# Second attention with score products of 64 rows: two maps side by side instead of stacked halves

## The chip, the cores and the metric

The kernel runs on one core of one Trainium2 chip. The metric is the device time of one execution in microseconds; the time before is 2244.63 us, the median of three runs (2244.57 to 2247.15).

## The reference

Two layers over 1024 tokens of width 1024, in float32. The first layer mixes tokens with latent attention, the second with differential attention; each mixer and each feed-forward block is followed by a layer norm. The change touches the differential attention alone:

```python
# 8 heads, two maps (m) of 64 columns each, values of 128 columns
q = q.reshape(b, s, 8, 2, 64); k = k.reshape(b, s, 8, 2, 64); v = v.reshape(b, s, 8, 128)
logits = einsum('bqhmd,bkhmd->bmhqk', q_b, k) * 64 ** -0.5 - slopes * dist      # then the chunk mask
p = softmax(logits)
a = p[:, 0] - lam * p[:, 1]
o = einsum('bhqk,bkhe->bqhe', a, v)
```

The mask lets a query see its own chunk of 64 tokens and all earlier ones.

## The kernel before, in words

Products of float32 numbers are made from "hi" and "lo" parts in the type fp32r: a number is cast (hi, on ScalarE), the rest is what the cast lost (lo, on VectorE), and a product is hi·hi + hi·lo + lo·hi. Most of the kernel is projections and feed-forward products of this kind with 128 rows and 512 columns.

The second attention is the `with ExitStack() as st` block from about line 1536 on. `attention` walks over 64 blocks, a head `h` and 128 queries `i` each, the last head in the order `LAST_ORDER`. For each it calls the scores two blocks ahead (`score_b`), then the transposes of the probabilities (`turn_b`), and after every second block the product with the values (`mix_b`). Other work is spread between by slot numbers (`at`, `fill`): the projections of the next head (`proj_b`, tile `bp`), values (`values_b`, tile `bv`), norms, and the first products of the output projection (`zp_a`). The order on each engine is then made by a planner, which runs a timeline of its own and takes the priorities of `tc.high_priority` into account; `behind(i, j)` holds two instructions of one engine in a given order.

`proj_b` makes 512 columns of the queries or keys of one head: 24 products into a bank of tag `m` (two banks), rows 0 to 63 for map 0 and 64 to 127 for map 1. The split out of this bank differs for queries and keys:

- Queries (L1592 to L1596): for each map, ScalarE casts its 64 rows into a tile of its own, VectorE makes the lo rows, and a DMA issued by GpSimd copies the 64 hi rows to the other 64 rows of the tile. So each map has a tile with hi in both halves, and a tile (`ql`) with lo in one half and zeros in the other. The zeros come once from DRAM (`zero_dr`, L1552), where the first attention stored them (`store_zeros`, L1492 and L1493).
- Keys (L1602, L1603): for each map, ScalarE casts its 64 rows into its own rows of the map's tile, and VectorE writes the lo part into the other 64 rows.

`score_b` then calls `softmax_block` once for each map. With n = 128(i+1) keys, in one bank of tag `s` where n is 512 or less and in two banks of n/2 columns where it is more, each bank takes two products of 128 rows (L241): [hi; hi] with [hi; lo], and [lo; 0] with the same keys. VectorE then adds the distances out of the bank and takes the row's bound (L244), ScalarE takes the exponential with its sum (L247), VectorE the reciprocal (L249). GpSimd scales map 1 (L1617) and VectorE joins the two maps (L1618). Three banks have the tag `s`, two `m`, two `t` (transposes), one `o`.

Of the kernel before, what the change touches and what calls it, by code (L numbers as in the profile page):

```python
# [9 lines left out]
F32 = mybir.dt.float32  # L10
F32R = mybir.dt.float32r
AF = mybir.ActivationFunctionType
ALU = mybir.AluOpType
# [3 lines left out]
P = 128  # L17
S = 1024
# [16 lines left out]
BIGF = 3.0e38  # L35
# [7 lines left out]
def trunk(  # L43
# [32 lines left out]
    nc = tc.nc  # L76
    V, A, G, T = nc.vector, nc.scalar, nc.gpsimd, nc.tensor
# [9 lines left out]
    wp = ctx.enter_context(tc.tile_pool(name="wp", bufs=3))  # L87
# [13 lines left out]
    dr = ctx.enter_context(tc.tile_pool(name="dr", bufs=1, space=DRAM))  # L101
# [7 lines left out]
    def f32(t):  # L109
        return t.bitcast(F32)  # L110

    def big_tile(name, dt=F32R):
        return big.tile([P, 2, 1024], dt, tag="big", name=name)

    def ps_s(name):
        return ps.tile([P, 512], F32, tag="s", bufs=ps_bufs[0], name=name)

    def ps_m(name):
        return ps.tile([P, 512], F32, tag="m", bufs=ps_bufs[1], name=name)
# [14 lines left out]
    def small(name, n=1):  # L134
        return sp.tile([P, 2], F32, tag="small", name=name, bufs=22)[:, :n]
# [3 lines left out]
    def load_w(src, cols, name, hi=None, lo=None, eng=None, raw=None, after=()):  # L139

        if raw is None:
            raw = wp.tile([P, 1024], F32, tag="wr", bufs=2, name=f"r_{name}")
        newest["weight load"] = nc.sync.dma_start(raw[:, :cols], src).ins
        if hi is None:
            hi = wp.tile([P, 1024], F32R, tag="wh", name=f"h_{name}")
            lo = wp.tile([P, 1024], F32R, tag="wl", name=f"l_{name}")
        i = A.copy(hi[:, :cols], raw[:, :cols])
        j = (eng or G).tensor_tensor(lo[:, :cols], raw[:, :cols], f32(hi[:, :cols]), ALU.subtract)
        for k, key in zip((i, j), after):
            behind(k.ins, newest[key])  # L150
        newest["weight"] = i.ins
        return hi, lo
# [14 lines left out]
    def mm3(ps_out, pairs):  # L167
        n = len(pairs)
        for i, (lh, ll, rh, rl) in enumerate(pairs):
            T.matmul(ps_out, lh, rh, start=(i == 0), stop=False)  # L170
            T.matmul(ps_out, lh, rl, start=False, stop=False)  # L171
            T.matmul(ps_out, ll, rh, start=False, stop=(i == n - 1))  # L172
# [9 lines left out]
    def behind(i, j):  # L182

        tc.add_manual_dep(
            i, j.name,
            mybir.DependencyInfo(mybir.DependencyClass.NoSync, mybir.DependencyReason.DATA),
            reason="kept in program order",
        )
# [42 lines left out]
    def softmax_block(lp, q_pass, s_bias, i, scale, name):  # L231
        n = (i + 1) * P
        nb = 1 if n <= 512 else 2
        w = n // nb
        l = lp.tile([P, 1024], F32, tag="l", name=f"l_{name}")
        mx = BIGF
        for b in range(nb):
            s = ps_s(f"s_{name}_{b}")
            ks = slice(b * w, (b + 1) * w)
            for j, (lh, rh) in enumerate(q_pass):  # L240
                T.matmul(s[:, :w], lh, rh[:, ks], start=(j == 0), stop=(j == len(q_pass) - 1))  # L241
            bv = s_bias[:, 896 - P * i + b * w:896 - P * i + (b + 1) * w]
            m = small(f"mx_{name}_{b}")
            V.tensor_tensor_reduce(l[:, ks], s[:, :w], bv, -scale, mx, ALU.add, ALU.min, m)  # L244
            mx = m
        sm = small(f"sm_{name}")
        newest["exp"] = A.activation(l[:, :n], l[:, :n], AF.Exp, bias=mx, scale=-1.0, accum_out=sm).ins  # L247
        r = small(f"r_{name}")
        V.reciprocal(r, sm)  # L249
        return l, r  # L250
# [953 lines left out]

    o_dr = [dr.tile([H, P, 256], F32, name=f"o_dr_{g}") for g in range(4)]
    on_dr = dr.tile([H - 2, P, 2, S], F32, name="on_dr")
    zero_dr = dr.tile([P, 512], F32, name="zero_dr")
    wo_dr = [dr.tile([P, 2, D], F32, name=f"wo_dr{h}") for h in range(H)]
    xs_dr = [dr.tile([S, D], F32, name=f"xs_dr{l}") for l in range(3)]

# [6 lines left out]
    ba, cos, sin = (krp.tile([P, S], F32, tag=t, name=t) for t in ("ba", "cos", "sin"))  # L1217
# [7 lines left out]
    with tc.tile_pool(name="a0", bufs=2, side="right") as pool:  # L1225
# [42 lines left out]
        kt = pool.tile([P, NTB, P], F32, tag="kt", name="kt", bufs=1)  # L1268
# [84 lines left out]
    with ast as st:  # L1353
        pool = st.enter_context(tc.tile_pool(name="a1", bufs=2, reuse_waits="tile"))
        vp = st.enter_context(tc.tile_pool(name="a1v", bufs=12, side="right", reuse_waits="tile"))
        lp = st.enter_context(tc.tile_pool(name="a1l", bufs=4, side="right", reuse_waits="tile"))
# [104 lines left out]
        def at(slot, fn, *args):  # L1461
            fill.setdefault(slot, []).append(lambda: fn(*args))
# [9 lines left out]
        for h in range(1, H):  # L1472
            b = 8 * (h - 1)
# [13 lines left out]
        at(10, load_late)  # L1487
        at(12, make_late)

        def store_zeros():  # L1490
            t = wp.tile([P, 1024], F32R, tag="wl", name="zeros")
            A.copy(t[:, :512], ba[:, :512])  # L1492
            nc.sync.dma_start(zero_dr, f32(t[:, :512]))  # L1493

        at(14, store_zeros)
        first = FirstBlock(w_o_a, o_dr)
        for h in range(first.HEADS):
            at(8 * H - 8 + h // 2, first.weight, h)
        tb, n = first.tb, first.HEADS
# [37 lines left out]
    with ExitStack() as st:  # L1537
        lp = st.enter_context(tc.tile_pool(name="b1l", bufs=5, reuse_waits="tile"))
        pool = st.enter_context(tc.tile_pool(name="b1", bufs=2, reuse_waits="tile"))
        ptp = st.enter_context(tc.tile_pool(name="b1p", bufs=4, reuse_waits="tile"))  # L1540
        bb = pool.tile([P, S], F32, tag="bb", name="bb", bufs=1)
        nc.sync.dma_start(bb, c_bias_b)
        vt, lt, pts, sqs, q_slot = {}, {}, {}, {}, {}
        qt = [big_tile(f"bq{j}") for j in range(2)]
        kt = [big_tile(f"bk{j}") for j in range(2)]
        ob = big_tile("bo", F32)
        q_hi = [qt[0][:, 0], qt[0][:, 1], qt[1][:, 0]]
        q_lo = [qt[1][:, 1]] + [pool.tile([P, S], F32R, tag=f"ql{j}", name=f"ql{j}", bufs=1) for j in range(2)]
        for ql in q_lo:
            for mp in range(2):  # L1550
                b = slice(64 - mp * 64, 128 - mp * 64)
                nc.sync.dma_start(f32(ql[b, mp * 512:mp * 512 + 512]), zero_dr[b])  # L1552

        def values_b(pr, tb):
            if ("v", pr) not in wts:
# [20 lines left out]
        def proj_b(h, which, hf):  # L1576
            if (which, h) not in wts:
                wts[which, h] = load_w(w_b_qk[h, which], 1024, f"wb{h}_{which}")
            wh, wl = wts[which, h]
            hs = slice(hf * 512, hf * 512 + 512)  # L1580
            m = ps_m(f"bp{h}_{which}_{hf}")
            mm3(m, [(wh[:, k * P:k * P + P], wl[:, k * P:k * P + P], xT[0][hf][:, k, :], xT[1][hf][:, k, :])
                    for k in range(KD)])
            sc = float(2.0 ** (h + 1) / 8.0)
            if which == 0:
                j = 2 * h + (hf if h < H - 1 else 1 - hf)
                q2, ql = q_slot[h, hf] = q_hi[j % 3], q_lo[j % 3]
                for mp in range(2):
                    a = slice(mp * 64, mp * 64 + 64)
                    b = slice(64 - mp * 64, 128 - mp * 64)  # L1590
                    qh = q2[:, mp * 512:mp * 512 + 512]
                    A.activation(qh[a], m[a, :], AF.Copy, scale=sc)  # L1592
                    V.scalar_tensor_tensor(
                        ql[a, mp * 512:mp * 512 + 512], m[a, :], sc, f32(qh[a]), ALU.mult, ALU.subtract
                    )
                    nc.gpsimd.dma_start(qh[b], qh[a])  # L1596
            else:
                for mp in range(2):
                    a = slice(mp * 64, mp * 64 + 64)
                    b = slice(64 - mp * 64, 128 - mp * 64)  # L1600
                    k = kt[h % 2][:, mp]
                    A.copy(k[a, hs], m[a, :])  # L1602
                    V.tensor_tensor(k[b, hs], m[a, :], f32(k[a, hs]), ALU.subtract)  # L1603

        def score_b(h, i):
            c = slice((i % 4) * P, (i % 4) * P + P)
            n = (i + 1) * P
            (q2, ql), k = q_slot[h, i // 4], kt[h % 2]
            (l0, r0), (l1, r1) = [
                softmax_block(  # L1610
                    lp,
                    [(t[:, m * 512:m * 512 + 512][:, c], k[:, m]) for t in (q2, ql)],
                    bb, i, float(2.0 ** -(h + 1)), f"b{h}_{i}_{m}",
                )
                for m in range(2)
            ]
            G.tensor_scalar(l1[:, :n], l1[:, :n], r1, nlam, ALU.mult, ALU.mult)  # L1617
            V.scalar_tensor_tensor(l0[:, :n], l0[:, :n], r0, l1[:, :n], ALU.mult, ALU.add)  # L1618
            lt[h, i] = l0
# [73 lines left out]
        for h in range(1, H):  # L1693
            b = 8 * (h - 1)
# [22 lines left out]
        b = 8 * (H - 1) - 2  # L1717
# [104 lines left out]
```

## Time and profile before

| | before |
|---|---|
| median of three runs | 2244.63 us |
| the profiled execution | 2244.52 us |
| its span in the profile | 2242.6 us |
| TensorE matmul busy | 2227.4 us (99%) |
| VectorE, ScalarE, GpSimd busy | 1587.6, 1008.6, 883.8 us |
| second attention, first to last score product | 1115.9 to 1524.9 us |

The span runs from the first to the last instruction that the profile records; the profiled execution's own time has 1.9 us beside it. PE is a row of matmuls, PEld one of weight loads, each load going ahead of its matmul. A matmul's duration in the profile runs from its start to the end of its last result, and the next one starts before that, so the cost of a matmul in a dense stretch is the distance between two starts, not its duration.

### The profile page before, as it was taken

The numbers are of one execution on the slowest core, as the hardware profiler recorded it, in microseconds if no ns is written. First come the engines' busy times: TensorE is split into PE (matmuls) and PEld (weight loads), VectorE is DVE, ScalarE is ACT, GpSimd is POOL, SyncE is SP. The second block draws the span as 40 slices with busy tenths as digits, with TensorE's granted clock in tenths as the row PEclk, the third lists the DMA queues.
The fourth block names the chain that finished last, engine by engine and source line by source line (L and its number), as shares of the span: only waits on it lengthen the run. The fifth ranks groups of instructions, "written<-read, shape, count | busy, mean of one in ns | idle before, by whom it ended". The sixth has DMA issues, their size and how long they took to land.

```text
span 2242.6 us, 30084 instructions
## 1 busy us (share of the span) xinstructions
PE 2227.4 (99%) x10850; PEld 1878.7 (84%) x10850; DVE 1587.6 (71%) x2951; ACT 1008.6 (45%) x2082; POOL 883.8 (39%) x711
## 2 busy tenths in 40 slices
PE   9999999999999999999999999999999999999998
PEld 9888888888888888888888888888888888888887
DVE  6677776597656667768588777776597666668668
ACT  4465664342323324445466656555442233334444
POOL 2243452015434446456433434321024444446452
PEclk9999999999999999999999999999999999999999
DMA  5031335334313138544310212164444232246644
GB/s 208 15 127 64 116 108 195 125 141 151 121 71 141 71 122 333 207 173 155 118 48 34 71 45 69 47 244 146 151 153 168 74 113 99 101 151 260 238 140 158
DMA packets 107989, 295.49 MB, mean 132 GB/s; under 512 B 8512, under 2 KB 34880, under 8 KB 96576
## 3 DMA queue, kind: packets, MB, share of 16 engines
q1 hardware_dynamic: 103552, 283.87, 35.9%
q0 software_dynamic: 4000, 9.44, 1.5%
q8 instruction: 86, 1.41, 0.3%
q14 instruction: 63, 0.52, 0.1%
q10 hardware_dynamic: 288, 0.26, 0.0%
HBM read 208.86 MB, written 80.48 MB: 129 GB/s over the span
## 4 chain that ended last, share of the span: by engine, by line
PE 95%; DVE 3%; ACT 1%; issue 1%; POOL 0%; DVEq 0%; ACTq 0%; POOLq 0%
PE gb L619 16%; PE ga L619 11%; PE gc L619 11%; PE dw L972 7%; PE dx L972 5%; PE zp_a L494 4%; PE s_a L241 3%; PE zp_a L351 3%; PE dv L972 3%; PE dy L972 3%; PE s_b L241 2%; PE bv L1564 2%; PE bp L170 2%; PE bp L172 2%; PE bp L171 2%; PE hq L1282 2%
## 5 line engine op out<-in xcount | busy, mean ns | idle before, releaser
L575 ACT CAST op_g<-gr 128x512 fp32r<-128x512 f32 x240 | 147.6, 622 | 400.2 <-PE gb L619 219.6
L575 POOL TENSOR_TENSOR op_g<-gr,op_g 128x512 fp32r<-128x512 f32 x104 | 147.2, 1421 | 304.8 <-DVE tmp L733 167.5
L575 DVE TENSOR_TENSOR op_h<-rh,op_h 128x512 fp32r<-128x512 f32 x154 | 156.2, 1029 | 86.8 <-ACT op_h L575 86.6
L619 PE MATMUL ga<-xh_m,op_g 128*128 128x512 f32 x512 | 168.1, 389 | 0.0
L972 PE MATMUL dw<-op_w_t,op_h 128*128 128x512 f32 x660 | 152.4, 391 | 0.0
L972 PEld LDWEIGHTS dw<-op_w_t,op_h 128*128 128x128 f32 x660 | 123.4, 188 | 25.6 <-POOL op_w_t L575 0.2
L575 ACT CAST op_h<-rh 128x512 fp32r<-128x512 f32 x154 | 92.3, 619 | 112.3 <-PE dv L972 34.6
L247 ACT ACTIVATE l_b<-l_b,mx_b 128x256 f32<-128x256 f32 (+7 forms) x128 | 99.5, 777 | 67.7 <-DVE mx_b L244 63.6
L575 POOL TENSOR_TENSOR op_w_t<-tt,op_w_t 128x512 fp32r<-128x512 f32 x66 | 93.7, 1420 | 89.9 <-ACT op_w_t L575 82.8
L1617 POOL TENSOR_SCALAR l_b<-l_b,r_b,cst 128x128 f32<-128x128 f32 (+3 forms) x64 | 52.9, 826 | 180.3 <-DVE r_b L249 150.2
L972 PE MATMUL dx<-op_w_b,op_h 128*128 128x512 f32 x528 | 120.3, 389 | 0.0
L575 DVE TENSOR_TENSOR op_g<-gr,op_g 128x512 fp32r<-128x512 f32 x136 | 110.6, 815 | 8.8 <-ACT op_g L575 8.6
L972 PEld LDWEIGHTS dx<-op_w_b,op_h 128*128 128x128 f32 x528 | 99.1, 188 | 20.6
L575 POOL TENSOR_TENSOR op_g<-s,op_g 128x512 fp32r<-128x512 f32 x40 | 56.6, 1414 | 150.1 <-ACT op_g L575 150.1
L619 PE MATMUL gc<-t1h_f,op_g 128*128 128x512 f32 x352 | 115.5, 389 | 0.0
L619 PE MATMUL gb<-t4h_f,op_g 128*128 128x512 f32 x352 | 115.5, 389 | 0.0
L619 PE MATMUL gc<-b22h_f,op_g 128*128 128x512 f32 x352 | 115.5, 389 | 0.0
L619 PE MATMUL gb<-t3h_f,op_g 128*128 128x512 f32 x352 | 115.2, 389 | 0.0
L619 PE MATMUL gb<-t2h_f,op_g 128*128 128x512 f32 x352 | 114.9, 389 | 0.0
L619 PEld LDWEIGHTS ga<-xh_m,op_g 128*128 128x128 f32 x512 | 96.1, 188 | 20.0
L170 PE MATMUL bp<-xT_f,h_wb 128*128 128x512 f32 x256 | 103.0, 403 | 1.0 <-DVE bk L1603 0.8
L172 PE MATMUL bp<-xT_f,l_wb 128*128 128x512 f32 x256 | 101.4, 396 | 0.0
(406 smaller groups left out, 6516.4 us busy)
## 6 DMA issues: line engine op xcount, KB each, us to landing
gr<-in_w_gu SPq DMA_DIRECT2D x44, 1024.0 KB, 6.9
rh<-h_dr SPq DMA_DIRECT2D x28, 1024.0 KB, 4.9
h_dr<-sh SPq DMA_DIRECT2D x22, 1024.0 KB, 4.9
h_dr<-hp SPq DMA_DIRECT2D x22, 768.0 KB, 4.0
tt<-in_w_dn SPq DMA_DIRECT2D x22, 512.0 KB, 8.4
rh<-h_dr SPq DMA_DIRECT2D x14, 768.0 KB, 4.3
z<-xs_dr SPq DMA_DIRECT2D x16, 512.0 KB, 11.2
rw_b<-in_w_dn SPq DMA_DIRECT2D x8, 1024.0 KB, 7.2
```

The source lines that it names most:

```text
L170: T.matmul(ps_out, lh, rh, start=(i == 0), stop=False)
L171: T.matmul(ps_out, lh, rl, start=False, stop=False)
L172: T.matmul(ps_out, ll, rh, start=False, stop=(i == n - 1))
L241: T.matmul(s[:, :w], lh, rh[:, ks], start=(j == 0), stop=(j == len(q_pass) - 1))
L247: newest["exp"] = A.activation(l[:, :n], l[:, :n], AF.Exp, bias=mx, scale=-1.0, accum_out=sm).ins
L351: i = T.matmul(m, ot[:, a, h, :], wo[h][w][:, c], start=(h == 0 and (a, w) == (0, 0)), stop=(h == H - 1 and a == 1), skip_group_check=True ...
L494: T.matmul(m, a[:, h, :], self.wo[h][w][:, c], start=(start and h == heads[0] and a is oh and w == 0), stop=(stop and h == heads[-1] and a ...
L575: return A.copy(hi, src).ins, eng.tensor_tensor(lo, src, f32(hi), ALU.subtract).ins
L619: T.matmul(o, w[:, a, kc], x[b][:, k, :], start=(first and k == 0 and (a, b) == (0, 0)), stop=(k == 3 and a == 1), skip_group_check=True,)
L972: i = T.matmul(o, h[:, a, c], w[:, b_], start=(first and (a, b_) == (0, 0)), stop=(last and a == 1), skip_group_check=True,).ins
L1282: T.matmul(hq[:, :384], lh[:, kc], w[:, 0:384], start=st, stop=sp_)
L1617: G.tensor_scalar(l1[:, :n], l1[:, :n], r1, nlam, ALU.mult, ALU.mult)
```

## The change

The queries and keys of both maps are split with all 128 rows at once: one cast on ScalarE and one operation on VectorE where there were two of each, hi and lo lying side by side in the free dimension. There are no second copies of the hi rows, no copying DMAs, and no zeros.

The score products become products of 64 rows: rows 0 to 63 are map 0, rows 64 to 127 map 1. Each map takes hi·hi, hi·lo and lo·hi, so a bank takes three products in place of two. Two banks of tag `s`, one for each map, are filled together, map 1 and map 0 by turns. `behind` keeps the six products in this order, and all but the first have a raised priority, so that the planner does not put other work between them. VectorE empties both banks, and the exponentials come when both maps are through. `softmax_block` is no longer used here; its steps stand in `score_b`.

```diff
-    zero_dr = dr.tile([P, 512], F32, name="zero_dr")
...
-        def store_zeros():
-            t = wp.tile([P, 1024], F32R, tag="wl", name="zeros")
-            A.copy(t[:, :512], ba[:, :512])
-            nc.sync.dma_start(zero_dr, f32(t[:, :512]))
-        at(14, store_zeros)
...
-        q_hi = [qt[0][:, 0], qt[0][:, 1], qt[1][:, 0]]
-        q_lo = [qt[1][:, 1]] + [pool.tile([P, S], F32R, tag=f"ql{j}", name=f"ql{j}", bufs=1) for j in range(2)]
-        for ql in q_lo:
-            for mp in range(2):
-                b = slice(64 - mp * 64, 128 - mp * 64)
-                nc.sync.dma_start(f32(ql[b, mp * 512:mp * 512 + 512]), zero_dr[b])
+        qt = [t[:, :, :512] for t in qt] + [pool.tile([P, 2, 512], F32R, tag="q", name="q", bufs=1)]
...
             if which == 0:
                 j = 2 * h + (hf if h < H - 1 else 1 - hf)
-                q2, ql = q_slot[h, hf] = q_hi[j % 3], q_lo[j % 3]
-                for mp in range(2):
-                    a = slice(mp * 64, mp * 64 + 64)
-                    b = slice(64 - mp * 64, 128 - mp * 64)
-                    qh = q2[:, mp * 512:mp * 512 + 512]
-                    A.activation(qh[a], m[a, :], AF.Copy, scale=sc)
-                    V.scalar_tensor_tensor(
-                        ql[a, mp * 512:mp * 512 + 512], m[a, :], sc, f32(qh[a]), ALU.mult, ALU.subtract
-                    )
-                    nc.gpsimd.dma_start(qh[b], qh[a])
+                q = q_slot[h, hf] = qt[j % 3]
+                A.activation(q[:, 0], m, AF.Copy, scale=sc)
+                V.scalar_tensor_tensor(q[:, 1], m, sc, f32(q[:, 0]), ALU.mult, ALU.subtract)
             else:
-                for mp in range(2):
-                    a = slice(mp * 64, mp * 64 + 64)
-                    b = slice(64 - mp * 64, 128 - mp * 64)
-                    k = kt[h % 2][:, mp]
-                    A.copy(k[a, hs], m[a, :])
-                    V.tensor_tensor(k[b, hs], m[a, :], f32(k[a, hs]), ALU.subtract)
+                k = kt[h % 2][:, :, hs]
+                A.copy(k[:, 0], m)
+                V.tensor_tensor(k[:, 1], m, f32(k[:, 0]), ALU.subtract)
...
         def score_b(h, i):
...
-            (l0, r0), (l1, r1) = [
-                softmax_block(lp, [(t[:, m * 512:m * 512 + 512][:, c], k[:, m]) for t in (q2, ql)],
-                    bb, i, float(2.0 ** -(h + 1)), f"b{h}_{i}_{m}")
-                for m in range(2)
-            ]
+            for b in range(nb):
+                ks = slice(b * w, (b + 1) * w)
+                ss = [ps_s(f"s_{nm}_{m}_{b}") for m in both]
+                last = None
+                for x, y in ((0, 0), (0, 1), (1, 0)):
+                    for m in (1, 0):
+                        a = slice(64 * m, 64 * m + 64)
+                        with tc.high_priority(0 if last is None else 200):
+                            one = T.matmul(ss[m][:, :w], q[a, x, c], k[a, y, ks], start=(x + y == 0), stop=(x == 1)).ins
+                        if last is not None:
+                            behind(one, last)
+                        last = one
+                for m in both:
+                    x = small(f"mx_{nm}_{m}_{b}")
+                    V.tensor_tensor_reduce(ls[m][:, ks], ss[m][:, :w], bv, -scale, mx[m], ALU.add, ALU.min, x)
+                    mx[m] = x
+            for m in both:
+                A.activation(ls[m][:, :n], ls[m][:, :n], AF.Exp, bias=mx[m], scale=-1.0, accum_out=sm)
+                V.reciprocal(rs[m], sm)
```

More of the change, by code (lines that the diff above doesn't have):

```diff
@@ L1607, in score_b @@
             n = (i + 1) * P
-            (q2, ql), k = q_slot[h, i // 4], kt[h % 2]
-            (l0, r0), (l1, r1) = [
[L1610 to L1614, printed above, removed]
-                for m in range(2)
-            ]
+            q, k = q_slot[h, i // 4], kt[h % 2]
+            nb = 1 if n <= 512 else 2
+            w = n // nb
+            scale, nm = float(2.0 ** -(h + 1)), f"b{h}_{i}"
+            both = range(2)
+            ls = [lp.tile([P, 1024], F32, tag="l", name=f"l_{nm}_{m}") for m in both]
+            mx = [BIGF, BIGF]
+            for b in range(nb):
[10 more added lines that the diff above has]
+                        last = one
+                bv = bb[:, 896 - P * i + b * w:896 - P * i + (b + 1) * w]
+                for m in both:
+                    x = small(f"mx_{nm}_{m}_{b}")
+                    V.tensor_tensor_reduce(ls[m][:, ks], ss[m][:, :w], bv, -scale, mx[m], ALU.add, ALU.min, x)
+                    mx[m] = x
+            rs = []
+            for m in both:
+                sm = small(f"sm_{nm}_{m}")
+                A.activation(ls[m][:, :n], ls[m][:, :n], AF.Exp, bias=mx[m], scale=-1.0, accum_out=sm)
+                rs.append(small(f"r_{nm}_{m}"))
+                V.reciprocal(rs[m], sm)
+            (l0, l1), (r0, r1) = ls, rs
             G.tensor_scalar(l1[:, :n], l1[:, :n], r1, nlam, ALU.mult, ALU.mult)
```

## The prediction

> **What bounds the kernel now.** The page comes first: busy time, clock and the chain.
>
> ```profile
> span 2242.6 us, 30084 instructions
> PE 2227.4 (99%) x10850; PEld 1878.7 (84%) x10850; DVE 1587.6 (71%) x2951; ACT 1008.6 (45%) x2082; POOL 883.8 (39%) x711
> PEclk9999999999999999999999999999999999999999
> PE 95%; DVE 3%; ACT 1%; issue 1%; POOL 0%; DVEq 0%; ACTq 0%; POOLq 0%
> ```
>
> TensorE is the bound: 99% busy at full clock, and 95% of the chain. The second view is the stretch of the second attention by engine, then its score products alone, then what PE waited for in it.
>
> ```profile
> core 0: us, PE busy (x) PEld busy (x) DVE busy (x) ACT busy (x) POOL busy (x), PEclk, DMA share, GB/s
> 1115.00:1531.00 416.00, 411.80 (x2173) 347.21 (x2172) 321.31 (x873) 255.72 (x591) 152.87 (x158) 1.00 0.24 80
> ...
> 1115.00:1531.00 416.00, 102.07 (x384) 65.57 (x384) 108.82 (x192) 1.00 0.24 80
> ...
> PE s_b L241 <- DVE mx_b L244: 2.1, 3, 0.9
> PE bp L170 <- DVE bk L1603: 0.8, 1, 0.8
> ```
>
> In 416 us PE is idle for 4.2 us. What the change does to other engines can give back no more than about that; its worth is decided by the room that 384 score products take on PE. Busy time overstates it, since durations overlap: the distance between starts counts. It is read from the timeline, at pairs and runs of score products.
>
> ```profile
> 1115.94 0.84 PE L241 MATMUL s_b<-bk,bq 128*128 128x128 f32 x6
> 1116.62 0.39 PE L170 MATMUL bp<-xT_f,h_wb 128*128 128x512 f32 x1
> ...
> 1120.95 0.40 PE L241 MATMUL s_b<-bk,bq 128*128 128x256 f32 x2
> 1121.19 0.40 PE L171 MATMUL bp<-xT_f,h_wb 128*128 128x512 f32 x1
> ...
> 1122.35 0.51 PE L241 MATMUL s_b<-bk,bq 128*128 128x384 f32 x2
> 1122.69 0.40 PE L170 MATMUL bp<-xT_f,h_wb 128*128 128x512 f32 x1
> ...
> 1383.98 0.39 PE L241 MATMUL s_b<-bk,bq 128*128 128x512 f32 x1
> 1384.21 0.40 PE L241 MATMUL s_b<-bk,ql 128*128 128x512 f32 x1
> ...
> 1386.27 0.30 PE L241 MATMUL s_b<-bk,bq 128*128 128x320 f32 x1
> 1386.41 0.31 PE L241 MATMUL s_b<-bk,ql 128*128 128x320 f32 x1
> 1386.56 0.40 PE L172 MATMUL bp<-xT_f,l_wb 128*128 128x512 f32 x1
> ```
>
> Between starts lie 0.23 us for 512 columns, 0.17 for 384, 0.145 for 320 (0.29/2), 0.12 for 256 (0.24/2) and 0.113 for 128 (0.68/6). Down to 256 columns that is proportional to the columns, so 0.20 for 448; 128 cost nearly as much as 256, so there is a floor of about 0.11 us for one load and its product.
>
> A head has one bank per map of 128, 256, 384 and 512 columns, and two each of 320, 384, 448 and 512 (the halves of 640 to 1024). With two products, two maps and eight heads, 32 for each bank: 96 of 512, 64 of 448, 96 of 384, 64 of 320, 32 of 256, 32 of 128, together 384, as the view counted. Their room: 22.1 + 12.8 + 16.3 + 9.3 + 3.8 + 3.6 = 67.9 us.
>
> **The change, part by part.** *Streams.* A pair of banks (one for each map) took four products of 128 rows and takes six of 64. If the products of the two maps, on different rows of the array, run side by side, six take the room of three: 67.9/4 = **17.0 us saved**. If they run one after another, six take that of six: 67.9/2 = 34.0 us lost. The trace of before has no product of 64 rows; these are the two ends. I take the first: the two maps have separate rows, separate banks and no common operand, and nothing in the rows above is a limit that both share, except the load floor.
>
> *Loads.* If the loads of the two maps can't overlap, a pair needs at least 2 × 0.113 = 0.226 us, just the room of 512 columns. There are 12 banks per map and head, so 96 pairs of banks of three steps: 96 × 3 × 0.226 = 65.1 us, 2.8 saved. I take it that they overlap, as the products do, and keep this end.
>
> *Changing between 64 and 128 rows.* The six products stand among products of 128 rows: 2 × 96 = 192 changes. What a change costs is the disputed term. The trace shows changes of another kind:
>
> ```profile
> 1331.72 0.32 PE L241 MATMUL s_b<-bk,bq 128*128 128x320 f32 x1
> 1331.87 0.49 PE L175 MATMUL pt_b<-ident,l_b 128*128 128x128 f32 x3
> ```
>
> A product of 320 columns gives way to transposes after 0.15 us, the plain price of its columns: a change of operation alone costs nothing. That is the lower end, 0. For the upper end, let the array run empty before the next kind begins: a product of 512 columns lasts 0.39 us and the next starts after 0.23, so 0.16 us of each is a tail that normally lies under the next. 192 × 0.16 = **30.7 us**. If the new weights, too, can only be loaded once it is empty, the load floor comes on top, 192 × (0.16 + 0.11) = 51.8 us, and with the whole load of 0.19 us 67.2. I take the tail, 30.7. The row of the transposes, where nothing is lost, is a change of what the array does with 128 rows; here the rows over which it adds are split and joined, and sums on the way through would be of the wrong kind. Loads now go ahead of the running product (the next load begins 0.01 us after its start), and I see no reason why that should end.
>
> ```profile
> 1115.71 0.39 PE L172 MATMUL bp<-xT_f,l_wb 128*128 128x512 f32 x1
> 1115.72 0.19 PEld L241 LDWEIGHTS s_b<-bk,bq 128*128 128x128 f32 x1
> ```
>
> On this very point the Trainium skill, TensorEngine Tiling (Array Packing), section Tiling Modes, states that a change of the tiling mode drains TensorE, while a change of tile within a mode does not; it names no time, and no row here shows such a change. By it the sum would be the one I take, or the one with the reload; without it, the faster rival below.
>
> *Splits.* The rows of the splits out of the projections, for 64 rows, and of the same work on 128:
>
> ```profile
> L1592 ACT ACTIVATE bq<-bp x32: 576/593/595, 1086.9 to 1461.2; 64x512 fp32r<-64x512 f32 x32
> L1602 ACT CAST bk<-bp x32: 566/582/585, 1110.7 to 1480.6; 64x512 fp32r<-64x512 f32 x32
> L1603 DVE TENSOR_TENSOR bk<-bp,bk x32: 683/688/695, 1111.3 to 1481.4; 64x512 fp32r<-64x512 f32 x32
> ...
> L1416 DVE TENSOR_TENSOR ql<-qn,qh x16: 670/688/692, 79.7 to 310.0; 128x512 fp32r<-128x512 f32 x16
> ...
> L575 ACT CAST op_g<-gr 128x512 fp32r<-128x512 f32 x240 | 147.6, 622 | 400.2 <-PE gb L619 219.6
> ...
> L1596 POOL DMA_DIRECT2D bq<-bq x32: 509/571/595, 1087.8 to 1462.9; - x32
> ```
>
> 128 rows cost VectorE what 64 do (688 ns) and ScalarE 622 for 582 to 593. VectorE: 64 operations of 0.688 become 32, 22.0 us less. ScalarE: 32 × 0.593 + 32 × 0.582 - 32 × 0.622 = 17.7 us less. GpSimd loses 32 issues of 0.571, 18.3 us, and the copies with them. All three engines lie under PE: 321, 256 and 153 us busy in 416. What reaches PE is the 4.2 us that it waits, 0.8 of it for the keys' split: I take **2.0 saved**, with 0 and 4.2 as the ends.
>
> *Zeros.* Six loads and one store on SP's queue and a cast of the first attention go. They stand ahead of work that PE isn't waiting for (the clock and the 95% above); 0.
>
> *Two banks at once.* Of three banks a pair takes two, so the next pair waits until VectorE has emptied map 0 of the last. Behind that wait stands all of PE. VectorE takes this long for a bank:
>
> ```profile
> L244 DVE CUSTOM_DVE_ANT_0 l_b<-s_b,bb x128: 263/553/692, 1116.3 to 1525.7; 128x384 f32<-128x384 f32 x32, 128x512 f32<-128x512 f32 x32, 128x128 f32<-128x128 f32 x16, 128x256 f32<-128x256 f32 x16
> ```
>
> For the 32 second pairs of the wide blocks that is at most 32 × (0.16 + 0.65) = 26 us, if nothing stands between, and 0 if four products of 0.23 us do. Between blocks there is enough (2173 matmuls for 64 blocks, 34 a block). The bank waited for longest belongs to the first product of a pair (map 1), so that no pair is torn. I take 0.
>
> *Later exponentials.* Map 0's exponential now waits for map 1's banks too, by one or two reductions, some 0.6 to 1.3 us. Scores run two blocks ahead, 2 × 416/64 = 13 us, so it is covered; without that lead the transposes would wait.
>
> **Sum.** -17.0 + 30.7 - 2.0 = +11.7 us. The profiled execution took 2244.5 us, its span 2242.6 and 1.9 around it, 0.1 from the median. 2244.5 + 11.7 = **2256**.
>
> **Rivals.** *No price for the change of rows (faster).* Rows are kept apart by group, each waits only for its own, and the array never empties: -17.0 - 2.0 = -19.0, 2225.5. For it: the transposes' row, 0. Against it: a sum over 128 rows has to become two. It decides once a change costs under (17.0 + 2.0)/192 = 0.10 us. The Trainium skill, TensorE: Matmul & The Clock Gate, Part 3, The mechanism, says that products on different row groups start some 4 ns apart, with loads overlapping; that would give this rival's streams, and no run here shows it.
>
> *Drain and reload.* Weights can't go ahead over a change: 51.8 - 19.0 = +32.8, 2277, and up to 67.2 - 19.0 = +48.2, 2293 with the whole load. Against it: every load in the timeline goes ahead.
>
> *The products don't overlap (the change doesn't do what it says).* 34.0 - 2.0 = +32.0, 2276.5 with free changes; 2307 with the tail. For it: no two matmuls of before ever share the array.
>
> *Only the loads don't overlap.* -2.8 - 2.0 = -4.8, 2239.7, if changes are free; +25.9, 2270, with the tail.
>
> *The banks.* The planner leaves second pairs right behind the first: +11.7 + 26 = 2282.
>
> **Chances.** Tail 0.40; no price 0.27; reload 0.13; no overlap of products 0.07; loads 0.06, half of it with free changes; banks 0.07. The likeliest is 2256; its own range, for a price between 0.07 and 0.22 us and a relief from 0 to 4.2, is 2239 to 2270. Both signs hold much, so the range goes from the free change, 2225, to 2290: left out are changes cheaper still with more relief, the full reload, and no overlap with tails, under 0.2. What this kernel's measurement can tell is about 0.2%, 4.5 us. Faster: 0.27 + 0.03, and 0.04 from cheap tails, 0.34. Same: 0.08, tails near 0.10 us. Slower: 0.58.
>
> **What would show it.** Forms 64*128 at the new score line, 576 of them, and 64x512 gone from the splits, with 128x512 at about 0.69 and 0.62 us. Right: starts of map 1 and map 0 a few hundredths apart, three steps of 0.23 us for 512 columns, and a gap of 0.16 us beyond the columns ahead of the first 64-row product and ahead of the next one of 128. Wrong: no such gap (faster), a load that only starts when the last product ends (reload), starts 0.23 us apart within a pair (no overlap), or PE waiting at score products for VectorE's reductions by more than 4 us (banks).

## The result, and the profile after

The changed kernel took 2305.57 us (2303.8 to 2306.34), the one before 2244.8 on the same chip: 1.0267 times as long, interval 1.0249 to 1.0285, or +60.8 us. The prediction was 2256 with a range to 2290; the sign was right, the size not.

The first three rows come from the page of the kernel after: span, busy time, and the chain by engine.

```profile
span 2302.0 us, 30178 instructions
...
PE 2266.1 (98%) x11042; PEld 1871.6 (81%) x11042; DVE 1564.5 (68%) x2919; ACT 984.0 (43%) x2048; POOL 869.9 (38%) x679
...
PE 94%; DVE 3%; ACT 1%; issue 1%; POOL 0%; DVEq 0%; ACTq 0%; POOLq 0%
```

PE has 38.7 us more of busy time in a span that is 59.4 us longer, so about 20 us of the loss are time in which PE does nothing. Where this lies is seen in busy time by stage, from the start of the second attention to its last score product and from there to the end, first of before, then of after.

```profile
1115.00:1526.00 411.00, 406.80 (x2149) 343.09 (x2148) 317.32 (x860) 251.88 (x580) 151.59 (x156) 1.00 0.24 77
1526.00:2242.00 716.00, 708.75 (x3160) 586.36 (x3158) 494.50 (x699) 269.26 (x494) 281.65 (x204) 1.00 0.43 153
```

```profile
1115.00:1581.00 466.00, 443.64 (x2334) 333.90 (x2334) 292.34 (x821) 227.73 (x545) 138.74 (x127) 0.98 0.18 61
1581.00:2302.00 721.00, 710.54 (x3168) 587.57 (x3166) 498.94 (x709) 270.78 (x500) 282.69 (x205) 1.00 0.42 151
```

The stage grew from 411 to 466 us: 55 of the 59.4. The granted clock, 1.00 before, is 0.98 there. VectorE, ScalarE and GpSimd all have less to do, as the change says. What PE waited for in the stage, and who waited for the score products' banks (from the answer on that tile):

```profile
PE s_b L1601 <- DVE mx_b L1608: 10.9, 11, 2.7
PE pt_b L175 <- DVE l_b L1618: 10.0, 8, 1.8
PE o_b L279 <- DVE pt_b L267: 1.6, 4, 0.6
...
  DVE l_b L1608: 36.3, 30
```

PE waited 22.9 us in all, against 3.9 before by the same view: half of it at score products, for VectorE's emptying of their banks (L1608), and most of the other half at transposes, for the joined probabilities (L1618). VectorE in turn waited 36.3 us for score products; before it was 14.5. Each waits for the other by turns.

The products' own price is read at a run of six between products with the values, in the timeline of PE.

```profile
1342.79 0.28 PE L280 MATMUL o_b<-pt_b,bvl 128*128 128x256 f32 x1
...
1343.01 0.96 PE L1601 MATMUL s_b<-bk,bq 64*128 64x512 f32 x6
...
1343.90 0.50 PE L279 MATMUL o_b<-pt_b,bvh 128*128 128x512 f32 x1
1344.00 0.19 PEld L280 LDWEIGHTS o_b<-pt_b,bvl 128*128 128x128 f32 x1
...
1344.23 0.28 PE L280 MATMUL o_b<-pt_b,bvl 128*128 128x256 f32 x1
```

Six 64-row products of 512 columns take 0.89 us (1343.01 to 1343.90); four of 128 rows took 4 × 0.23 = 0.92. Three steps of 0.23 are 0.69, so the six do run two by two, and 0.20 is lost inside the run. Another 0.10 is lost ahead of it (0.22 from the product of 256 columns, where 0.12 is its room) and 0.10 behind it (0.33 where 0.23 is the room): 0.40 us for a run. The next load, of L280, starts 0.10 us after its predecessor's start and not 0.01. This is not a price of that one run: of the 113 runs of this trace, 67 have no wait, no lowered clock and no transpose beside them, and the same sum over each of them, with the room that the prediction read for every width, has a median of 0.40 us (mean 0.44).

The splits have the expected form and price; sixteen for the keys, and eleven of the sixteen for the queries stand under the tile's first name:

```profile
L1580 ACT CAST bk<-bp x16: 564/586/589, 1111.0 to 1530.6; 128x512 fp32r<-128x512 f32 x16
L1581 DVE TENSOR_TENSOR bk<-bp,bk x16: 678/692/693, 1111.6 to 1531.2; 128x512 fp32r<-128x512 f32 x16
...
L1576 ACT ACTIVATE bq<-bp x11: 588/597/600, 1087.1 to 1509.6; 128x512 fp32r<-128x512 f32 x11
```

Last, the three stretches of the kernel after in which the granted clock is halved (the column behind GpSimd's is the clock), each below the 3.41 us ahead of it.

```profile
1225.68:1229.09 3.41, 1.13 (x10) 0.84 (x10) 3.28 (x12) 1.89 (x8) 1.25 (x2) 1.00 0.01 2
1229.09:1232.50 3.41, 3.38 (x15) 2.52 (x14) 3.05 (x14) 2.19 (x8) 0.98 (x2) 0.50 0.00 0
1348.56:1351.97 3.41, 0.74 (x8) 0.55 (x10) 1.98 (x12) 3.14 (x8) 0.32 (x1) 1.00 0.00 0
1351.97:1358.79 6.82, 5.31 (x24) 3.87 (x25) 5.58 (x18) 3.54 (x13) 2.97 (x3) 0.50 0.00 0
1474.85:1478.26 3.41, 1.13 (x12) 0.67 (x10) 1.96 (x13) 3.41 (x12) 1.09 (x1) 1.00 0.00 0
1478.26:1485.09 6.83, 5.26 (x20) 4.19 (x21) 5.82 (x20) 3.85 (x13) 2.90 (x4) 0.50 0.00 0
```

At half clock they lose 1.7 + 3.4 + 3.4 = 8.5 us; counting only the time in which PE is busy, half of 3.38, 5.31 and 5.26, it is 7.0. Ahead of each, PE is busy for a third of the time or less. Just ahead of the second one PE runs dry, at the first, narrow blocks of a head:

```profile
1347.51 0.95 PE L175 MATMUL pt_b<-ident,l_b 128*128 128x128 f32 x7 [1.21 <-DVE l_b L1618]
1348.39 0.75 PE L1601 MATMUL s_b<-bk,q 64*128 64x128 f32 x6
...
1351.80 1.00 PE L1601 MATMUL s_b<-bk,q 64*128 64x256 f32 x6 [2.67 <-DVE mx_b L1608]
...
1354.32 1.94 PE L175 MATMUL pt_b<-ident,l_b 128*128 128x128 f32 x8 [1.51 <-DVE l_b L1618]
```

Score products wait for banks and transposes for probabilities, with next to no other work between. A pair takes two of three banks, so one and a half pairs are all the depth there is.

**The account.** In the trace of after the 576 products stand in 113 runs: 60 of six, 24 of five, 22 single ones, 5 of twelve, 2 of seven. The planner often sets a pair's first product apart, by itself or behind the run of the pair before it. So: streams -17.0 (the prediction's term), runs 113 × 0.40 = +45.2, idle time of PE in the stage (466.00 - 443.64) - (411.00 - 406.80) = +18.2, clock +7.0; together +53.4, where the stage grew by 55. With 0.35 for a run, the lower price of experiment two below, it is +47.8. The 4 to 5 us of the rest lie behind the stage (716 to 721) and are not explained. That sum uses prices read off the trace it explains; the experiments take the terms apart.

### The profile page after: what moved, and what is told of

Its sections match the earlier page's. It is cut to its first block, busy times and chain, and to the rows that moved or that the text cites. A ratio compares the mean times of both kernels' runs of the same rounds, so it can differ in the third digit from the quotient of the medians.

```text
span 2302.0 us, 30178 instructions
## 1 busy us (share of the span) xinstructions
PE 2266.1 (98%) x11042; PEld 1871.6 (81%) x11042; DVE 1564.5 (68%) x2919; ACT 984.0 (43%) x2048; POOL 869.9 (38%) x679
## 4 chain that ended last, share of the span: by engine, by line
PE 94%; DVE 3%; ACT 1%; issue 1%; POOL 0%; DVEq 0%; ACTq 0%; POOLq 0%
PE gb L619 16%; PE ga L619 10%; PE gc L619 10%; PE dw L972 7%; PE dx L972 5%; PE zp_a L494 4%; PE zp_a L351 3%; PE s_a L241 3%; PE s_b L1601 3%; PE bv L1552 3%; PE bp L170 3%; PE dv L972 3%; PE dy L972 3%; PE bp L171 3%; PE bp L172 3%; PE hq L1281 1%
## 5 line engine op out<-in xcount | busy, mean ns | idle before, releaser
L170 PE MATMUL bp<-xT_f,h_wb 128*128 128x512 f32 x256 | 103.9, 406 | 0.2 <-DVE edge L1558 0.2
L171 PE MATMUL bp<-xT_f,h_wb 128*128 128x512 f32 x256 | 101.4, 396 | 0.0
```

## The experiments

**One: the order of products alone.** From before: two banks at once, maps by turns, held in order with raised priority, exponentials after both maps; but products of 128 rows, splits and copies as before.

```diff
...
+                for x, t in enumerate((q2, ql)):
+                    for m in (1, 0):
+                        lh = t[:, m * 512:m * 512 + 512][:, c]
+                        with tc.high_priority(0 if last is None else 200):
+                            one = T.matmul(ss[m][:, :w], lh, k[:, m, ks], start=(x == 0), stop=(x == 1)).ins
+                        if last is not None:
+                            behind(one, last)
...
```

> The kernel before with the new order alone: products of 128 rows as before (queries doubled, lo padded with zeros, splits for each map), but the two maps by turns into two banks, four products held together with the raised priority, exponentials after both maps. No product of 64 rows. Theory 1, price of the change of rows: in the trace of after a run of 64-row products costs PE 0.43 us beyond its columns (0.09 to 0.10 before its first load, 0.10 after its last product, two loads of 0.107 that nothing covers), 113 runs, 48.5 us, less 17.0 for the streams; the rest is planner's noise. Then this run stands near before, 2245 to 2252. Theory 2, the order: the new order makes PE wait for VectorE (22.9 us in after, 4.2 before), and that is carried by banks taken in pairs, early first products and later exponentials. Then this run is 15 to 30 us slower than before, 2260 to 2275.

Measured: 2278.49 against 2245.36, +33.1 us (1.0148, 1.0133 to 1.0163). The stage, PE's waits in it, the bank's waiters and one dip:

```profile
1115.00:1556.00 441.00, 418.84 (x2153) 348.93 (x2152) 314.61 (x861) 246.45 (x579) 152.97 (x156) 0.98 0.22 72
...
PE pt_b L175 <- DVE l_b L1640: 8.1, 9, 1.6
PE s_b L1623 <- DVE mx_b L1630: 7.6, 13, 2.0
...
  DVE l_b L1630: 27.8, 23
...
1172.00:1182.00 10.00, 8.31 (x35) 7.26 (x36) 6.74 (x23) 5.46 (x19) 3.85 (x4) 0.66 0.06 13
```

The stage is 30 us longer without a single 64-row product, and the whole run 3 us slower than the slowest expected. PE waits 23.0 us, 19.1 more than before, 15.7 of them at the same two places, and the clock takes up to 6.8 (with two more dips of 0.83): some 25 of the 30. So the new order, with two of three banks filled together, has a price of its own, in size about half of the whole loss.

**Two: the rows alone.** From before, in its own order, one bank at a time: only the product with the lo part of the queries uses 64 rows (the other half was zeros).

```diff
-                    [(t[:, m * 512:m * 512 + 512][:, c], k[:, m]) for t in (q2, ql)],
+                    [(q2[:, m * 512:m * 512 + 512][:, c], k[:, m]),
+                     (ql[64 * m:64 * m + 64, m * 512:m * 512 + 512][:, c], k[64 * m:64 * m + 64, m])],
```

> The kernel before with one edit: the product of lo with the keys reads its own 64 rows alone instead of 128 with zeros. Same columns, same banks, same order of work around it; 192 products of 64 rows, one at a time, nothing runs beside them. Theory 1 (price): up to 192 runs of 0.43 us, 82 us, about 2327; if the planner sets two such products together, down to 96 runs, 41 us, 2286. Theory 2 (order) and the rival that a change of rows is free: 2245, no change.

Measured: 2312.82, +67.5 us (1.0300, 1.0285 to 1.0315). Stage, wait, and one such product in the timeline:

```profile
1115.00:1594.00 479.00, 478.35 (x2156) 345.13 (x2155) 317.24 (x862) 253.51 (x582) 150.66 (x156) 1.00 0.20 66
...
PE s_b L241 <- DVE mx_b L244: 0.7, 2, 0.4
...
1139.97 0.30 PE L241 MATMUL s_b<-bk,bq 128*128 128x320 f32 x1
1140.20 0.18 PEld L241 LDWEIGHTS s_b<-bk,ql 64*128 64x128 f32 x1 [0.28 <-issue]
1140.21 0.41 PE L241 MATMUL s_b<-bk,ql 64*128 64x320 f32 x1
1140.54 0.50 PE L171 MATMUL bp<-xT_f,h_wb 128*128 128x512 f32 x1
1140.88 0.40 PE L172 MATMUL bp<-xT_f,l_wb 128*128 128x512 f32 x1
```

PE is busy for 478.35 of 479 us, at full clock: what is lost here is the change of rows and nothing else. 0.24 us before the 64-row product and 0.33 behind it, where 0.145 is the room of 320 columns, and 0.34 behind the first product of 512, where 0.23 is: 0.10 + 0.19 + 0.11 = 0.40 us for one excursion of 64 rows, as in the run of six. For 192 of them that is 76.8; less the 3.5 us that PE no longer waits, that is 73, and 67.5 were measured (0.35 each, or 0.37 with those 3.5 added). The median over 167 such excursions of this trace, without waits or transposes beside them, is 0.40. Between 0.35 and 0.40 is what this price is known to. That lies between the 41 and 82 us that the price of a change was expected to come to; a free change is ruled out.

The first product after a change lasts longer, too: 0.41 for 320 columns in place of 0.30, and 0.50 for 512 in place of 0.40, as did L279 behind the run of six. That is about the load floor of 0.11, inside the product: its weights are not loaded ahead. So a change costs a gap of some 0.10 us ahead of the product, and 0.10 of a load inside it; the 0.19 is the load of the 64-row product and the gap behind it. By the records the load at 1140.20 starts 0.07 us before the product ahead ends (1139.97 + 0.30), so that the array is nearly empty by then; these ends are modelled, so whether it is wholly empty is not shown. The drain that the Trainium skill, TensorEngine Tiling (Array Packing), section Tiling Modes, states without a time fits this; the trace agrees, with 0.10 us of gap in the 0.20 of a change.

**Three: one map after the other.** From after, the loops over maps and products swapped, so that map 1's three products are issued ahead of map 0's.

```diff
-                for x, y in ((0, 0), (0, 1), (1, 0)):
-                    for m in (1, 0):
+                for m in (1, 0):
+                    for x, y in ((0, 0), (0, 1), (1, 0)):
```

> After with the six products of a run in another order: three of map 1, then three of map 0, so that neighbours share their rows. If products on different rows truly share the array, a run takes near six steps instead of three: 67.9 x 3/4 = 50.9 us more on PE, of which the 23 us of waits may hide a part: 2333 to 2357. If the overlap is only an appearance of the records: no change, 2306.

Measured: 2319.86, +74.5 on before (1.0332, 1.0314 to 1.0349), which is 14.3 us on after; with no overlap the streams alone would have cost 51 more (34.0 + 17.0). It lies between the two expectations, and looked as if overlap were small. The last experiment shows that it is not. In the trace of this run the planner made 128 runs of the 576 products, 77 of them of three, and PE waited 8.5 us in place of 22.9: fifteen more runs at 0.40 are 6.0, the second half of the torn pairs some 19 by the room of their columns, and the waits give 14.4 back, an estimate of 11 us of the 14.3.

**Four: the splits by halves.** From after, each split done for 64 rows at a time, twice.

```diff
-                A.copy(k[:, 0], m)
-                V.tensor_tensor(k[:, 1], m, f32(k[:, 0]), ALU.subtract)
+                for a in (slice(0, 64), slice(64, 128)):
+                    A.copy(k[a, 0], m[a, :])
+                    V.tensor_tensor(k[a, 1], m[a, :], f32(k[a, 0]), ALU.subtract)
```

(and the same for the queries)

> After with the splits of queries and keys made for each map again, 64 rows at a time: 32 more operations of 0.69 us on VectorE and 32 of 0.59 on ScalarE, the same values. By the prediction's term (2.0 us, 0 to 4.2) it is 0 to 4 us slower than after, 2306 to 2310. By theory 2, where VectorE is what PE waits for in after, more, 5 to 12 us, 2311 to 2318.

Measured: 2307.19, +61.8 (1.0276, 1.0261 to 1.0291): 1.6 us on after, with intervals that overlap. Some 40 us of work on VectorE and ScalarE come back and PE hardly notices; 2.0 was the prediction's term. The copies that GpSimd issued are not put back here, so their worth is not tested.

**Five and six: which part of the order.** From experiment one. The first leaves out the held order and the raised priority; the second writes each map's exponential right behind its own last reduction.

```diff
-                        with tc.high_priority(0 if last is None else 200):
+                        with tc.high_priority(0):
...
-                        if last is not None:
-                            behind(one, last)
```

> order_alone (2278.5 against 2245.4 of before) without the raised priority and without the order held among the four products of a pair of banks: banks in pairs and later exponentials stay. If priority or the held order make the 33 us: 2245 to 2252. If it is the pairs of banks, which make the planner use up the projections under the wide blocks so that PE runs dry at the narrow first blocks of a head: no change, 2268 to 2285.

```diff
+                    if b == nb - 1:
+                        sm = small(f"sm_{nm}_{m}")
+                        A.activation(ls[m][:, :n], ls[m][:, :n], AF.Exp, bias=mx[m], scale=-1.0, accum_out=sm)
+                        rs.append(small(f"r_{nm}_{m}"))
+                        V.reciprocal(rs[m], sm)
...
-            for m in both:
-                sm = small(f"sm_{nm}_{m}")
-                A.activation(ls[m][:, :n], ls[m][:, :n], AF.Exp, bias=mx[m], scale=-1.0, accum_out=sm)
-                rs.append(small(f"r_{nm}_{m}"))
-                V.reciprocal(rs[m], sm)
```

> order_alone with each map's exponential and reciprocal written right after that map's last reduction, map 0's ahead of map 1's reduction, as in the kernel before. If the later exponential of map 0 (one or two reductions, 0.6 to 1.3 us a block) is what PE waits for at the transposes (8.1 us in order_alone): 8 to 20 us faster than order_alone, 2258 to 2270. If it is the pairs of banks: no change, 2272 to 2285.

Measured: without held order and priority 2269.64, +24.4 (1.0110, 1.0095 to 1.0125), so these make some 9 of the 33 us; with early exponentials 2295.30, +50.0 (1.0223, 1.0207 to 1.0238), 17 us worse, outside both of its expectations. The rows of PE's waits at score products and transposes, first without held order, then with early exponentials:

```profile
PE s_b L1623 <- DVE mx_b L1628: 8.1, 7, 2.6
PE pt_b L175 <- DVE l_b L1638: 4.8, 7, 1.3
```

```profile
PE s_b L1623 <- DVE mx_b L1630: 21.2, 21, 1.8
PE pt_b L175 <- DVE l_b L1639: 4.4, 5, 1.4
```

So nothing is gained by writing the exponentials early. Written early, the reciprocals stand in VectorE's queue ahead of the reduction that would free a bank: VectorE's wait for exponentials ahead of reciprocals grows from 37.1 to 63.1 us, and PE's wait at score products from 7.6 to 21.2. Because the edit moves the reciprocals too, it does not clear the later exponentials by themselves. The larger part of the order's price, 24 us, is left with what the version without held order still has: the joint use of the banks and the later exponentials.

**Seven and eight: work kept for the narrow blocks.** From one and from after: the second projection of the keys of four heads is put behind the last score product issued by then, so that it lies under the narrow blocks, where PE runs dry.

```diff
+HELD = (1, 2, 4, 6)
...
+            first = T.matmul(ps_out, lh, rh, start=(i == 0), stop=False).ins
+            if i == 0 and after is not None:
+                behind(first, after)
...
-            for j, slot in enumerate((2, 3, 5, 6) if h < H - 1 else (1, 2, 3, 5)):
+            for j, slot in enumerate((2, 3, 5, 7 if h in HELD else 6) if h < H - 1 else (1, 2, 3, 5)):
```

> order_alone with one projection of the keys (24 products, 5.5 us on PE) in heads 1, 2, 4 and 6 held behind the head's second score block, so that it stands under the narrow first blocks, where PE ran dry. Theory of the dry stretches: the four of them cost waits of some 3 to 5 us and 3 us of lowered clock each, and most comes back: 10 to 25 us faster than order_alone, 2254 to 2268. If PE's waits only move to the wide blocks, from which the products were taken: 2272 to 2285.

> The same edit in the changed kernel (2305.6): by the theory of the dry stretches 10 to 25 us faster, 2281 to 2296, and still slower than before by the price of about 113 runs of 64-row products (0.35 us each in rows_alone, 40 us) less 17 for the streams. If the waits only move: 2300 to 2310.

Measured: 2284.32, +39.0 (1.0173, 1.0158 to 1.0188), and 2314.30, +69.0 (1.0308, 1.0290 to 1.0325); 6 and 8 us worse than the kernels they came from, the second slower than either expectation. The expected gain did not come: at score products PE now waits 17.7 us (14 times) in the first and 22.0 (18 times) in the second, where it was 7.6 and 10.9. Waits of 1.4 to 2.7 us at the blocks of 256 columns are still there, and new ones of 1.7 to 2.5 us stand at blocks of 448 columns. A projection kept for one place is missing in another, and the narrow blocks were not filled by it. This edit did not test the depth of the banks, which the next four do.

**Nine to twelve: the number of banks.** `PS_BUFS_B` gives the banks of the tags s, m, t and o. With four for s, the products with the values share the projections' banks; this has a price of its own, so before, one (the order alone) and after all get it. The fourth gives s two banks, and the third to the transposes, and leaves before's order.

```diff
-PS_BUFS_B = (3, 2, 2, 1)
+PS_BUFS_B = (4, 2, 2)
```

> The kernel before with PSUM banks of the second attention divided 4 for scores, 2 shared by projections and the products with values, 2 for transposes (3, 2, 1 and 2 before). The control for the next two: within 10 us of before, 2240 to 2255.

> order_alone (2278.5) with the same four score banks, so that a second pair of banks need not wait until map 0 of the first is emptied. If pairs in three banks make PE and VectorE wait for each other (PE waits 23.0 us, clock loss 6.8 us, VectorE waits 27.8 for score products against 14.5 in before): most of the 33 us goes, within 10 us of before_4banks. If it is the joint order of the two maps whatever the banks: 20 to 35 us above before_4banks.

> After (2305.6) with four score banks. By the theory of the pairs in three banks, the waits go and the price of the changes stays: some 20 to 30 us above before_4banks (113 runs x 0.35 less 17.0 = 23). By the other theory 50 to 65 us above it.

```diff
-PS_BUFS_B = (3, 2, 2, 1)
+PS_BUFS_B = (2, 2, 3, 1)
```

> The kernel before with two score banks instead of three (the third goes to the transposes), still one bank at a time. If the depth of the score banks is what counts, it loses as order_alone does, 15 to 35 us: 2260 to 2280. If only the joint order of the maps counts: within 8 us of before.

| kernel | us | on before | ratio, interval |
|---|---|---|---|
| before, four banks | 2269.13 | +24.5 | 1.0110, 1.0095 to 1.0125 |
| order alone, four banks | 2274.91 | +30.3 | 1.0133, 1.0118 to 1.0149 |
| after, four banks | 2265.30 | +20.7 | 1.0093, 1.0076 to 1.0110 |
| before, two banks | 2291.11 | +46.5 | 1.0206, 1.0191 to 1.0221 |

With four banks, two whole pairs, the order costs 30.3 - 24.5 = 5.8 us in place of 33.1 (the two intervals overlap), and after gets 40 us faster. The control missed its expectation: the new sharing costs before 24.5 us where 10 at most were expected, so these runs don't change the depth of the score banks alone. With two banks, before itself loses 46.5 us, more than the 35 expected, with nothing else changed than the third bank's use. The stage and PE's wait at score products of after with four banks, then of before with four, then of before with two:

```profile
1115.00:1546.00 431.00, 427.42 (x2352) 330.76 (x2351) 292.35 (x839) 231.57 (x557) 138.19 (x130) 0.99 0.20 69
...
PE s_b L1601 <- DVE mx_b L1608: 2.4, 1, 2.4
```

```profile
1115.00:1546.00 431.00, 412.07 (x2135) 343.00 (x2134) 316.73 (x857) 251.39 (x578) 150.31 (x156) 0.99 0.24 78
...
PE s_b L241 <- DVE mx_b L244: 8.2, 9, 2.6
```

```profile
1115.00:1569.00 454.00, 429.20 (x2146) 353.70 (x2145) 316.04 (x861) 254.01 (x580) 150.76 (x156) 0.96 0.22 71
...
PE s_b L241 <- DVE mx_b L244: 16.9, 29, 1.3
```

A single wait at score products is left of the eleven in after, and before shows the wait of after as soon as its banks are short. So too few banks are enough for these waits and for the dips behind them, and in the changed kernel two whole pairs take nearly all of them away. Depth is not all that counts: before with four banks waits 8.2 us at score products, where it waited 2.1 with three, so the sharing of the other banks has waits of its own.

After with four banks was expected 20 to 30 us above its control and came out 3.8 below it. It has 80 runs and not 113, and 80 × 0.40 less 17.0 for the streams is +15.0; but PE idles only 431.00 - 427.42 = 3.6 us where the control idles 18.9. So the changed rows still cost some 15 us here by this sum, and the waits of the control hide it. After with four banks is the fastest version with 64 rows; its interval overlaps that of its control, so the 3.8 us are not shown as a gain. None of the kernels here beats before.

**Thirteen: one map after the other, with four banks.** Experiment three again, where waits don't cover what the array does.

> after_4banks (2265.3; 80 runs of 64-row products, PE waits about 4 us) with the six products in the order of serial_maps, three of map 1, then three of map 0. Without waits to hide it, the loss of the overlap shows: up to 3/4 of 67.9 = 50.9 us, less what two adjoining products of different maps still share: 2300 to 2316. If the overlap saves little and serial_maps' 14 us were its whole worth: 2275 to 2285.

Measured: 2274.94 against 2245.41, +29.5 (1.0129, 1.0111 to 1.0147), 9.6 us on after with four banks by difference of medians. By its time alone that is what was expected if the overlap saved little; the timeline of PE, at two runs, says otherwise:

```profile
1261.86 0.97 PE L1601 MATMUL s_b<-bk,q 64*128 64x512 f32 x6
1262.76 0.50 PE L172 MATMUL bp<-xT_f,l_wb 128*128 128x512 f32 x1
1263.20 0.96 PE L1601 MATMUL s_b<-bk,q 64*128 64x512 f32 x3
1264.09 0.50 PE L170 MATMUL bp<-xT_f,h_wb 128*128 128x512 f32 x1
```

The program as built has this order on PE here (block, map and bank last; all of head 2):

```
s_b_7_1_0 x3, s_b_7_0_0 x3, bp (L172), s_b_7_1_1 x3, bp (L170)
```

Three products of map 1 and then three of map 0 take 0.90 us, as many as by turns, and three of map 1 alone take 0.89: the second map is free whatever the order within a run. Without overlap six would have taken 3 × 0.23 = 0.69 us more. What costs is a pair that is torn, since it needs two excursions; 29 runs of three are in this trace, 89 runs in all against 80. Nine runs at 0.40 are 3.6 us, and the second half of the torn pairs is some 9 by the room of its columns, an estimate of 13 us where 9.6 were measured. So the small loss of experiment three did not speak against overlap.

## Why the prediction was wrong

- **Streams, -17.0: right.** Six products take three steps, and starts of the two maps lie mostly 3 to 4 ns apart in the trace, loads too. The rule cited for the faster rival, of the Trainium skill, TensorE: Matmul & The Clock Gate, Part 3, The mechanism (starts some 4 ns apart, loads overlapping), agrees with this. Both rivals without overlap fall. The same section has matmuls go strictly in the program's order; there the runs differ: 0.90 us for three of one map followed by three of the other.
- **Changing between 64 and 128 rows, +30.7: mis-sized, +45 (+40 at 0.35).** The step that failed is "I take the tail, 30.7", with "I see no reason why that should end" of loads that go ahead. The gap is 0.10 and not 0.16, but the load does not go ahead over a change, 0.10 more: 0.20 for a change, 0.40 for an excursion (0.35 by the sum of experiment two). So "drain and reload" had the mechanism, with too long a tail. And there are 226 changes (113 runs), not 192: "no pair is torn" did not hold, since the planner leaves first products apart.
- **Two banks at once, 0: wrong, about +25.** The step was "Between blocks there is enough (2173 matmuls for 64 blocks, 34 a block). ... I take 0." That is a mean over blocks. The work between is used up under the wide blocks, and at a head's narrow first blocks there is next to none (the dry stretch above). 18.2 us of idle time and 7.0 of clock are what came of it, and the order alone cost 33.1 in experiment one; the upper bound of 26 was near, though it was reckoned for second pairs of wide blocks. The fall of the clock after waits was no term of the sum.
- **Splits, -2.0: right within what can be told** (1.6 in experiment four; the operations at 0.69 and 0.59). VectorE and ScalarE got less work and it was worth little; what GpSimd's copies were worth was not tested. **Zeros, 0** and **later exponentials, 0**: nothing in the traces speaks against, but neither was tested by itself; with exponentials and reciprocals written earlier it got worse.
- **The range.** Each rival was priced alone beside the forecast. Drain and reload together with banks would have been -17.0 + 51.8 + 26 - 2.0 = +58.8, or 2303, near the 2305.6; both have causes that don't exclude each other, yet the range ended at 2290. That the sum fits so well is partly chance, as its terms are off by 7 (45 for 51.8). A slip beside it: with a price of 0.07 us and a relief of 4.2 the forecast's own range would begin at 2237, not at 2239; nothing rests on it.

Open remain the 4 to 5 us behind the stage, the 4 to 5 us of experiment one's stage beyond waits and clock, and what in the shared banks costs before 24.5 us.

## What to carry to other kernels

Putting products on half the rows pays only by the stretch: an excursion out of 128 rows costs 0.35 to 0.40 us here whatever its length, so the 17 to 19 us that this change saves would have paid for some 43 to 54 runs, where there were 113; runs of two blocks together would be needed, which wasn't tried. Buffers taken in pairs halve the depth of their pool: three banks hold one and a half pairs, and whether work covers a wait is read at the poorest place of the loop (here the first blocks of a head), not from the mean. When two rivals in a prediction don't exclude each other, price them together too, and let the range reach there.

## What was not expected of the hardware

- Weights that are first after a change of rows are not loaded ahead; their load starts 0.07 us before the recorded end of the product ahead. It makes 0.20 us for a change and 0.40 for an excursion, the same for one product of 320 columns and for six of 512.
- Products on different rows need not stand by turns in the program: 0.90 us for three and three, 0.89 for three alone.
- The clock falls though PE never waits longer than 2.7 us at a stretch: it was half for 3.41, 6.82 and 6.83 us in after, and 0.96 over the whole stage with two banks, where no wait was longer than 1.3 us. The Trainium skill, TensorE: Matmul & The Clock Gate, Part 1, What's actually happening, puts half speed behind an idle window of some 3.4 us; here the 3.41 us ahead of each fall held 1.13, 0.74 and 1.13 us of short products, so waits of 2.7 us and less with short products between them were enough.
